# One fixed order from the first loads to the first values, a larger VectorE share of the modulation, and RMS norms two tiles at a time

## The chip, the cores and the metric

The kernel runs on one core of one Trainium2 chip. The metric is device time in microseconds (us) of one launch, from runs on the chip; less is better. The core has five instruction queues that run in order and meet through semaphores: TensorE (PE), VectorE (DVE), ScalarE (ACT), GpSimd (POOL) and SyncE (SP, which here issues most of the transfers).

## The reference, cut to what matters

A hybrid decoder block on `x` (1, 2048, 1024) in float32. The part at issue is its beginning:

```python
c_act = silu(c)                                   # (1, 1024)
mod = c_act @ w_mod + b_mod                       # (1, 3072): shift, scale, gate
h = rms_norm(x, g_norm) * (1.0 + scale) + shift   # (2048, 1024)
proj = h @ w_in                                   # 8 x 1024 columns, "v" among them
```

After that come a causal convolution with a gated linear recurrence, an attention of three dilated windows, a gated merge, an output projection with a gated residual, and a last RMS norm.

## The kernel before, in words

Positions are handled in four banks of 512 (`x0`, `x1` and so on, each four tiles of 128 rows by 1024 columns), two banks to a half `f`. Channels are on partitions in `h` (eight blocks `k` of 128), so every block of `x` is normed by rows, transposed on PE against an identity matrix and then scaled and shifted by a per-partition `gs` and `sh`. Products are made from three matmuls each (`mm3`): operands are split into a rounded part ("hi", written by ACT) and the rest ("lo", a subtraction on DVE or POOL), and hi*hi + hi*lo + lo*hi are added up in PSUM.

The stages of the first half are: the prologue (norm of `x0`, modulation, the operands `B11` and `B21` made of `x0`); the "values" (`v` = `h @ w_in` for four column groups `m` of 256 and the two banks, 96 matmuls of 128x256 for each group and bank; the norm of `x1` and its operands are made meanwhile); a long stage with the recurrence, the gates and the other projections; then the same for the second half; then attention and the output.

The prologue works in four steps `j`, each of 256 columns of shift (`q` = 0) and scale (`q` = 1):

- `load_mod(j)` loads two tiles of 1 MB (`w_m[q, j]`, eight input blocks by 256 columns) on the SP queue.
- For the first `KV` of the eight input blocks DVE multiplies the block by its column of `ca` (silu of `c`) and adds it to `acc` (one `tensor_scalar`, then `scalar_tensor_tensor`, L607 and L609). The other blocks go to PE as matmuls of one output row (`X<-T,ca`), and one more matmul with a column of ones adds up `acc` over the partitions (`X<-acc,ones`).
- ACT copies that row to SBUF (`mrow`, L615), four tiny matmuls turn it into columns (`pg<-ones,mrow`), and DVE makes `mod` (L627) and `gs` (L628) of it.
- `build` for the blocks `k` = 2j and 2j+1: four transposes on PE (L489), hi and a full copy `hf` on ACT (L492, L495), lo on DVE (L163).

Ahead of the steps are 30 idle matmuls on `busy`, the transpose of all small parameters (`prow` to `par`, L567, L568), the sigmoid of `c` (L571), and `norm_x`, which for each of the four tiles does a sum of squares on ACT, `rstd` (small operations on DVE and a square root on ACT) and the scaling by it on DVE (L478). 4, 4 and 10 more idle matmuls follow the turned rows of steps 0 to 2.

The order on each engine up to attention comes from a scheduler that works with a timeline of its own; `tc.issue_after(...)` ties some instructions behind others (L594, L603, L623, L633, L635, L637, L673). From attention on, `tc.manual_schedule()` takes the program's order. The weights of the values go through five raw buffers `R` (`NRAW`) and seven split buffers `S` (`NS`), hi by ACT (L154) and lo by POOL (L160).

Of the kernel before, what the change touches and what calls it, by code (L numbers as in the profile page):

```python
# [38 lines left out]
KV = 4  # L39
# [47 lines left out]
def decoder_block(ctx, tc, x, c, positions, g_norm, w_mod, b_mod, w_in, b_gate, conv_w, conv_b,  # L87
# [55 lines left out]
    last_mm = [None]  # L143

    def mm(o, l, r, st, sp, **kw):
        last_mm[0] = nc.tensor.matmul(o, lhsT=l, rhs=r, start=st, stop=sp, **kw).ins  # L146
# [18 lines left out]
    def rstd(ss):  # L165

        v, y, t = ss[:, 0:1], ss[:, 1:2], ss[:, 2:3]
        nc.vector.tensor_scalar(v, v, 1.0 / D, EPS, ALU.mult, ALU.add)
        nc.scalar.activation(y, v, AF.Sqrt)
        nc.vector.reciprocal(y, y)  # L170
# [33 lines left out]
    pair_id, last_hi, last_load, last_lo, last_copy = {}, [None], [None], [None], [None]  # L204
# [214 lines left out]

    def load_wv_half(m, k):  # L420

        wh = s_tile([P, KH, 2 * P])
        wl = s_tile([P, KH, 2 * P])
        for k2 in range(0, KH, 2):
            t = raw_tile([P, 2, 2 * P])
            rows = slice((k + k2) * P, (k + k2 + 2) * P)
            last_load[0] = nc.sync.dma_start(
                t[:], wcol(4 * D + m * 2 * P, 2 * P)[rows].rearrange("(k p) m -> p k m", p=P)).ins
            hi_act(wh[:, k2 : k2 + 2], t[:])
            lo_pool(wl[:, k2 : k2 + 2], t[:], wh[:, k2 : k2 + 2])  # L430
        return wh, wl
# [32 lines left out]
    def load_x(pool, n, tag, bufs):  # L464
        xs = []
        for r in range(0, 4, 2):
            t = T(pool, [P, 2, D], F32, tag, bufs=bufs)
            last_load[0] = nc.sync.dma_start(t[:], xv[n, r : r + 2].rearrange("r j d -> j r d")).ins
# [3 lines left out]
    def norm_x(st, xs, nb=2):  # L472
        for t in xs:
            jk = T(st, [P, D], BF16, "hf", bufs=nb)
            ss = T(st, [P, 4], F32, "ss", bufs=4)
            nc.scalar.activation(jk[:], t, AF.Square, accum_out=ss[:, 0:1])
            rstd(ss)
            nc.vector.tensor_scalar(t, t, ss[:, 1:2], None, ALU.mult)  # L478
# [3 lines left out]
    def build(st, names, xs, k, first=False, keep=None, spare=True):  # L482

        hh, hl = B[names[k // KH]]
        n_built[0] += 1

        pt = T(pj, [P, 4, P], F32, "Y") if spare and n_built[0] % 3 == 0 else T(pg, [P, 4, P], F32, "pg")
        for r in range(4):
            nc.tensor.transpose(pt[:, r, :], xs[r][:, k * P : (k + 1) * P], ident)  # L489
# [15 lines left out]
    def build_even(st, xs, ks=range(KT), first=False, spare=True):  # L505
        for k in ks:
            build(st, ("B11", "B21"), xs, k, first, spare=spare)
# [48 lines left out]
    idle_matmuls(30)  # L556
    nc.scalar.dma_start(cs[:], cst[:, :N_CST_A])
    prow = T(vx, [P, P], F32, "prow")

    rows = lambda v: v.rearrange("(k p) -> k p", p=P)  # L560
    for i, (r0, ap) in enumerate((
# [4 lines left out]
    pt = T(pg, [P, CH], F32, "pg")  # L566
    nc.tensor.transpose(pt[:, :N_PAR], prow[:N_PAR, :], ident[:N_PAR, :N_PAR])  # L567
    nc.vector.tensor_copy(par[:], pt[:, :N_PAR])  # L568

    ca = T(cp, [P, KT], F32, "ca")  # L570
    ca_act = nc.scalar.activation(ca[:], par[:, C_C : C_C + KT], AF.Sigmoid).ins  # L571
    nc.vector.tensor_tensor(ca[:], ca[:], par[:, C_C : C_C + KT], ALU.mult)

    norm_x(vx, x0)
    operand("B11")
    operand("B21")
# [5 lines left out]
    w_m, ws0 = {}, []  # L582
# [7 lines left out]
    for j in range(4):  # L590
        load_mod(j)
        if j == 1:

            with tc.issue_after(ca_act):  # L594
                ws0.append(load_wv_half(0, 0))
    pm_ins, gs_ins, acc_ins = [], [], []
    for j in range(4):


        pr = pj_tile([P, 2, 256])  # L600
        with ExitStack() as order:
            for ins in pm_ins[-1:] + gs_ins[-2:-1] + acc_ins[-1:]:
                order.enter_context(tc.issue_after(ins))  # L603
            for q in range(2):
                t = w_m[q, j]
                acc = T(vx, [P, 256], F32, "acc", bufs=4)
                nc.vector.tensor_scalar(acc[:], t[:, 0, :], ca[:, 0:1], None, ALU.mult)  # L607
                for k in range(1, KV):
                    acc_ins.append(nc.vector.scalar_tensor_tensor(acc[:], t[:, k, :], ca[:, k : k + 1], acc[:],  # L609
                                                                  ALU.mult, ALU.add).ins)  # L610
                for k in range(KV, KT):
                    mm(pr[:1, q, :], ca[:, k : k + 1], t[:, k, :], q == 0 and k == KV, False, skip_group_check=True)
                mm(pr[:1, q, :], ones[:, 0:1], acc[:], False, q == 1, skip_group_check=True)
        row = T(vx, [1, 2, 256], F32, "mrow", bufs=1)
        nc.scalar.activation(row[:], pr[:1], AF.Copy)  # L615
        pm = T(pg, [P, 2, 2], F32, "pg")
        for q in range(2):
            for i in range(2):
                mm(pm[:, q, i : i + 1], row[:, q, i * P : (i + 1) * P], ones[:1, 0:1],
                   q == 0 and i == 0, q == 1 and i == 1, skip_group_check=True)  # L620
        pm_ins.append(last_mm[0])
        if j < 3:
# [978 lines left out]
```

## Time and profile before

| | us |
|---|---|
| median of 3 runs | 2337.65 |
| lowest, highest | 2332.69, 2343.75 |
| the profiled execution | 2338.7 |
| its span | 2336.9 |
| PE busy in the span | 2246.0 (96%) |
| DVE, ACT, POOL busy | 1347.5, 1206.0, 952.1 |

The span runs from the first to the last recorded instruction, so 1.8 us of the profiled execution lie around it. Times in the rows below are from the start of the span. A row of the timeline has start and duration, engine, line, operation, output<-inputs, shape, count of instructions merged, and in brackets the idle time of the engine before it and what ended it. PEld is the loading of PE's stationary operand. A float32 matmul that the kernel issues once for `ca` or `ones` shows as two matmuls in the trace.

### The profile page before, as it was taken

The numbers are of one execution on the slowest core, as the hardware profiler recorded it, in microseconds if no ns is written. First come the engines' busy times: TensorE is split into PE (matmuls) and PEld (weight loads), VectorE is DVE, ScalarE is ACT, GpSimd is POOL, SyncE is SP. The second block draws the span as 40 slices with busy tenths as digits, with TensorE's granted clock in tenths as the row PEclk, the third lists the DMA queues.
The fourth block names the chain that finished last, engine by engine and source line by source line (L and its number), as shares of the span: only waits on it lengthen the run. The fifth ranks groups of instructions, "written<-read, shape, count | busy, mean of one in ns | idle before, by whom it ended". The sixth has DMA issues, their size and how long they took to land.

```text
span 2336.9 us, 34037 instructions
## 1 busy us (share of the span) xinstructions
PE 2246.0 (96%) x11461; PEld 1872.0 (80%) x11461; DVE 1347.5 (58%) x2442; ACT 1206.0 (52%) x2391; POOL 952.1 (41%) x734
## 2 busy tenths in 40 slices
PE   8998999899989999999999999999999898989998
PEld 4996777677777998787888877888889797978887
DVE  4737666756676534544434472366666777658443
ACT  4636656665643635555444411567768787634111
POOL 2456556665545533332211120446565656433000
PEclk9999999999999999999999999999999999999999
DMA  7375777676778759999677778989987887799532
GB/s 263 108 237 205 277 265 262 239 243 246 242 246 268 227 174 327 311 325 322 227 231 225 234 250 269 301 245 266 279 254 247 236 245 238 221 310 281 179 122 95
DMA packets 427284, 569.21 MB, mean 244 GB/s; under 512 B 71942, under 2 KB 292834, under 8 KB 426084
## 3 DMA queue, kind: packets, MB, share of 16 engines
q1 hardware_dynamic: 389268, 447.27, 62.2%
q10 hardware_dynamic: 37648, 119.70, 13.3%
q8 instruction: 91, 1.49, 0.3%
q14 instruction: 85, 0.70, 0.1%
q0 software_dynamic: 192, 0.05, 0.0%
HBM read 355.08 MB, written 211.82 MB: 243 GB/s over the span
## 4 chain that ended last, share of the span: by engine, by line
PE 50%; DMA 8%; DVE 4%; ACT 3%; issue 3%; POOL 2%; SPq 1%; ACTq 0%; POOLq 0%; DVEq 0%
PE pj L146 11%; PE pq L146 7%; PE X L146 6%; PE V L146 6%; PE o L146 4%; PE sc L146 4%; PE Z L146 3%; PE W L146 3%; PE Y L146 2%; PE pT L1217 1%; DMA wD<-s 1%; PE pT L1230 1%; PE pg L146 1%; DMA vraw<-vN 1%; DVE yl L163 1%
## 5 line engine op out<-in xcount | busy, mean ns | idle before, releaser
L146 PE MATMUL pj<-yh,S 128*128 128x512 f32 x1024 | 372.0, 408 | 6.1 <-DMA S<-wD 3.2
L146 PE MATMUL V<-T,S 128*128 128x512 f32 x1344 | 334.3, 397 | 12.0 <-ACT t L809 5.2
L160 POOL TENSOR_TENSOR S<-R,S 128x512 fp32r<-128x512 f32 x168 | 241.8, 1455 | 253.8 <-ACT S L200 79.2
L146 PE MATMUL X<-T,S 128*128 128x512 f32 x1344 | 332.4, 395 | 1.2 <-ACT t L888 1.2
L146 PEld LDWEIGHTS V<-T,S 128*128 128x128 f32 x1344 | 252.6, 189 | 75.9 <-ACT t L809 7.2
L146 PEld LDWEIGHTS X<-T,S 128*128 128x128 f32 x1344 | 252.4, 188 | 61.8 <-ACT t L888 2.1
L146 PEld LDWEIGHTS pj<-yh,S 128*128 128x128 f32 x1024 | 195.6, 191 | 44.0 <-DVE fg L1424 3.6
L146 PE MATMUL pj<-yl,S 128*128 128x512 f32 x512 | 203.0, 397 | 0.0
L1133 ACT ACTIVATE pp<-pp,st 128x256 f32<-128x256 f32 (+3 forms) x256 | 133.9, 524 | 113.4 <-DVE st L1132 112.7
L146 PE MATMUL W<-T,S 128*128 128x512 f32 x672 | 174.1, 404 | 0.0
L146 PE MATMUL Y<-T,S 128*128 128x512 f32 x672 | 168.6, 398 | 2.1 <-DVE t L418 2.1
L146 PE MATMUL Z<-T,S 128*128 128x512 f32 x672 | 167.4, 397 | 0.0
L146 PEld LDWEIGHTS W<-T,S 128*128 128x128 f32 x672 | 130.3, 194 | 32.4 <-issue 0.9
L146 PEld LDWEIGHTS Y<-T,S 128*128 128x128 f32 x672 | 127.0, 190 | 33.3 <-DVE t L418 2.5
L146 PEld LDWEIGHTS Z<-T,S 128*128 128x128 f32 x672 | 127.5, 190 | 30.2
L160 POOL TENSOR_TENSOR S<-s,S 128x512 fp32r<-128x512 f32 x84 | 114.9, 1369 | 77.7 <-ACT S L200 55.0
L163 DVE TENSOR_TENSOR ptl<-pT,pth 128x384 fp32r<-128x384 f32 (+1 forms) x160 | 97.8, 628 | 64.8 <-ACT pth L154 62.6
L1197 ACT ACTIVATE pp<-pp,M 128x256 f32<-128x256 f32 (+3 forms) x256 | 117.9, 523 | 8.7 <-DVE M L1321 8.6
L1132 DVE CUSTOM_DVE_ANT_0 pp<-sc,msk 128x256 f32<-128x256 f32 (+3 forms) x256 | 105.1, 449 | 30.0 <-PE sc L146 27.2
L779 DVE SCALAR_TENSOR_TENSOR xc<-xr,par,xc 128x512 f32<-128x512 f32 x96 | 84.8, 883 | 56.5 <-ACT xc L773 55.6
L160 POOL TENSOR_TENSOR kq<-kraw,kq 128x512 fp32r<-128x512 f32 (+1 forms) x64 | 101.1, 1590 | 22.9 <-ACT kq L154 22.9
L160 POOL TENSOR_TENSOR vh<-vraw,vh 128x256 fp32r<-128x256 f32 (+1 forms) x64 | 67.2, 1050 | 105.1 <-ACT vh L154 99.4
(358 smaller groups left out, 4697.7 us busy)
## 6 DMA issues: line engine op xcount, KB each, us to landing
sD<-S ACTq DMA_DIRECT2D x196, 512.0 KB, 4.2
S<-sD SPq DMA_DIRECT2D x196, 512.0 KB, 5.0
S<-wD SPq DMA_DIRECT2D x99, 512.0 KB, 5.5
R<-in_w_in_dram SPq DMA_DIRECT2D x136, 256.0 KB, 3.9
wD<-s ACTq DMA_DIRECT2D x64, 256.0 KB, 5.5
T<-in_w_mod_dram SPq DMA_DIRECT2D x8, 1024.0 KB, 11.5
vN<-ev SPq DMA_DIRECT2D x64, 128.0 KB, 2.7
zaT<-ev SPq DMA_DIRECT2D x32, 256.0 KB, 4.5
```

The lines of the kernel that those rows point to most:

```text
L146: last_mm[0] = nc.tensor.matmul(o, lhsT=l, rhs=r, start=st, stop=sp, **kw).ins
L160: nc.gpsimd.tensor_tensor(o, i, h.bitcast(F32), ALU.subtract)
L163: return nc.vector.tensor_tensor(o, i, h.bitcast(F32), ALU.subtract).ins
L779: nc.vector.scalar_tensor_tensor(xc, xr[:, i : i + CH], cw(i), xc, ALU.mult, ALU.add)
L1132: nc.vector.tensor_tensor_reduce(pdst, s_ps, mask, 1.0, 3e38, ALU.add, ALU.min, m_)
L1133: nc.scalar.activation(pdst, pdst, AF.Exp, bias=m_, scale=-1.0, accum_out=l_)
L1197: nc.scalar.activation(pp, pp, AF.Copy, scale=w)
L1217: nc.tensor.transpose(pt[:, c0 + j * P : c0 + (j + 1) * P], pp[i][:, k * P : (k + 1) * P], ident)
L1230: nc.tensor.transpose(pt[:, c * P : (c + 1) * P], pp[:, half * P : (half + 1) * P], ident)
```

## The change

1. `KV` goes from 4 to 5: of the eight input blocks of each modulation tile, DVE now sums five and PE three.
2. From the first idle matmuls to the end of the values of `m` = 0 of the first bank, the order on all engines is the program's (`tc.manual_schedule()`); the `issue_after` ties there are gone. The sums of a step for `q` = 0 come ahead of the builds of the step before, and those for `q` = 1 behind them; the transposes of step `j` stand between its row sums.
3. The values of `m` = 0 are issued in parts inside steps 2 and 3 (12, 12 and 24 matmuls for the first four blocks), and the other 48 behind the last step.
4. `c` alone is transposed first and its sigmoid taken between the squares of the first and the second pair of tiles; all parameters are transposed later. Idle matmuls are 16 and 8 instead of 30, 4, 4 and 10.
5. The raw loads of the value weights are issued apart from their splits; one more of them (`raws[1, 0]`) stands ahead of the first wait for a free buffer, and `x1` is loaded behind two more.
6. `norm_pair` takes one `rstd` for two tiles, in all places where `x` is normed. In `rstd`, one operation with two scalars and one with one become a product and an operation with two scalars.
7. The norm of `x1` is tied behind the last full copy of the prologue's builds.

```diff
-KV = 4
+KV = 5
...
-        nc.vector.tensor_scalar(t, t, v, -0.5, ALU.mult, ALU.mult)
-        nc.vector.tensor_scalar(t, t, 1.5, None, ALU.add)
+        nc.vector.tensor_tensor(t, t, v, ALU.mult)
+        nc.vector.tensor_scalar(t, t, -0.5, 1.5, ALU.mult, ALU.add)
...
+    def norm_pair(st, xs, nb=2):
+        ss = T(st, [P, 3, 2], F32, "ss", bufs=4)
+        for i, t in enumerate(xs):
+            jk = T(st, [P, D], BF16, "hf", bufs=nb)
+            nc.scalar.activation(jk[:], t, AF.Square, accum_out=ss[:, 0, i : i + 1])
+        rstd(ss)
+        for i, t in enumerate(xs):
+            nc.vector.tensor_scalar(t, t, ss[:, 1, i : i + 1], None, ALU.mult)
...
-    idle_matmuls(30)
...
+    def row_sums(j, q):
+        if q == 0:
+            pr[j] = pj_tile([P, 2, 256])
+        t = w_m[q, j]
+        acc = T(vx, [P, 256], F32, "acc", bufs=4)
+        nc.vector.tensor_scalar(acc[:], t[:, 0, :], ca[:, 0:1], None, ALU.mult)
+        for k in range(1, KV):
+            nc.vector.scalar_tensor_tensor(acc[:], t[:, k, :], ca[:, k : k + 1], acc[:], ALU.mult, ALU.add)
+        for k in range(KV, KT):
+            mm(pr[j][:1, q, :], ca[:, k : k + 1], t[:, k, :], q == 0 and k == KV, False, skip_group_check=True)
+        mm(pr[j][:1, q, :], ones[:, 0:1], acc[:], False, q == 1, skip_group_check=True)
...
+    with tc.manual_schedule():
+        idle_matmuls(16)
+        pc = T(pg, [P, CH], F32, "pg")
+        nc.tensor.transpose(pc[:, :KT], prow[:KT, :], ident[:KT, :KT])
+        cc = T(vx, [P, KT], F32, "cc")
+        nc.vector.tensor_copy(cc[:], pc[:, :KT])
...
+        squares(0)
+        nc.scalar.activation(ca[:], cc[:], AF.Sigmoid)
+        nc.vector.tensor_tensor(ca[:], ca[:], cc[:], ALU.mult)
+        rstd(norm[0])
+        scale_x(0)
+        squares(1)
+        idle_matmuls(8)
+        pt = T(pg, [P, CH], F32, "pg")
+        nc.tensor.transpose(pt[:, :N_PAR], prow[:N_PAR, :], ident[:N_PAR, :N_PAR])
+        nc.vector.tensor_copy(par[:], pt[:, :N_PAR])
+        rstd(norm[1])
+        row_sums(0, 0)
+        scale_x(1)
...
+        for j in range(4):
+            if j:
+                row_sums(j, 0)
+                build_x(j - 1)
+            if j == 2:
+                for k in range(0, KH, 2):
+                    split_wv(ws0[0], k, raws.pop((0, k)))
+                raws[1, 2] = load_wv_raw(1, 2)
+                raws[1, 4] = load_wv_raw(1, 4)
+                x1 = load_x(hp, 1, "T", 14)
+            if j == 3:
+                for k in range(KH, KT, 2):
+                    split_wv(ws0[1], k - KH, raws.pop((0, k)))
+                raws[1, 6] = load_wv_raw(1, 6)
+                first_values(0, 1, range(KH))
+            turn_x(2 * j)
+            row_sums(j, 1)
+            row(j)
+            turn_x(2 * j + 1)
+            if j == 2:
+                pv0 = [pj_tile([P, 2, 256]) for g in range(2)]
+                first_values(0, 0, range(KH))
+            if j == 3:
+                for r in range(2):
+                    first_values(1, r, range(KH))
+            turn_row(j)
+        build_x(3)
+        ws1 = [[s_tile([P, KH, 2 * P]) for l in range(2)]]
+        for k in range(0, KH, 2):
+            split_wv(ws1[0], k, raws.pop((1, k)))
+        for ks in (range(KH, KH + 2), range(KH + 2, KT)):
+            for g in range(2):
+                for r in range(2):
+                    first_values(g, r, ks)
...
+            for g in range(2):
+                store_values(vx, 0, n0, g, pv0[g])
+            with tc.issue_after(last_copy[0]):
+                norm_x(vx, xs)
```

`turn_x(k)` makes the four transposes of block `k`, `row(j)` the copy to `mrow`, `turn_row(j)` the four tiny matmuls, `mod` and `gs`, `build_x(j)` hi, `hf` and lo of the blocks 2j and 2j+1, `first_values(g, r, ks)` three matmuls for each block in `ks`.

More of the change, by code (lines that the diff above doesn't have):

```diff
@@ L503, in operand, with build_even @@
         B[name] = (slot(), slot())
-    def build_even(st, xs, ks=range(KT), first=False, spare=True):
+    def build_even(st, xs, ks=range(KT), spare=True):
         for k in ks:
-            build(st, ("B11", "B21"), xs, k, first, spare=spare)
+            build(st, ("B11", "B21"), xs, k, spare=spare)
     def build_odd(st, xs):
@@ L588, in load_mod, with turn_x, row, turn_row @@
             nc.sync.dma_start(t[:], w_mod[0, :, c0 : c0 + 256].rearrange("(k p) m -> p k m", p=P))
[L590 to L615, printed above, removed]
+    def row_sums(j, q):
[9 more added lines that the diff above has]
+        mm(pr[j][:1, q, :], ones[:, 0:1], acc[:], False, q == 1, skip_group_check=True)
+    def turn_x(k):
+        px[k] = turned(x0, k, T(pj, [P, 4, P], F32, "Y") if k % 2 else T(pg, [P, 4, P], F32, "pg"))
+    def row(j):
+        px["row"] = T(vx, [1, 2, 256], F32, "mrow", bufs=1)
+        nc.scalar.activation(px["row"][:], pr[j][:1], AF.Copy)
+    def turn_row(j):
         pm = T(pg, [P, 2, 2], F32, "pg")
```

133 lines of the change are left out of this document (73 added, 60 removed).

## The prediction

> **What bounds the kernel now.** I read the page's busy shares first, then busy time in stretches of 60 us, then the timeline of the first 100 us engine by engine, and last the clock around PE's longer pauses. The stretches have start and end, length, busy time and count of PE, PEld, DVE, ACT and POOL, the granted clock, the DMA share and GB/s.
>
> ```profile
> PE 2246.0 (96%) x11461; PEld 1872.0 (80%) x11461; DVE 1347.5 (58%) x2442; ACT 1206.0 (52%) x2391; POOL 952.1 (41%) x734
> ...
> 0.00:60.00 60.00, 52.41 (x275) 29.41 (x276) 30.23 (x84) 29.20 (x48) 14.68 (x19) 0.94 0.79 262
> 60.00:120.00 60.00, 58.33 (x489) 57.67 (x488) 44.19 (x100) 39.54 (x70) 24.38 (x15) 1.00 0.40 113
> ```
>
> PE is busy for 96% of the span, 52.4 of the first 60 us and 58.3 of the next. So time gained or lost in the prologue goes, for the most part, to the end one for one: all that follows is fed by PE's stream. The change touches some 70 of 2337 us, and 0.5% of the time, about what a measurement of this kernel can tell from no change, is 11.7 us.
>
> What does PE do in the prologue, and from when is it useful?
>
> ```profile
> 1.46 9.44 PE L146 MATMUL V<-busy 128*128 128x512 bf16 x30 [1.46 <-DVE htail L724]
> 17.45 3.52 PE L146 MATMUL X<-T,ca 128*1 128x256 f32 x8 [0.82 <-DVE ca L572]
> 21.25 1.89 PE L146 MATMUL X<-T,ca 128*1 128x256 f32 x8
> 28.35 0.59 PE L146 MATMUL Z<-acc,ones 128*1 128x256 f32 x2
> 39.31 0.66 PE L489 MATMUL Y<-cs,T 128*128 128x128 f32 x4
> 40.12 1.05 PE L146 MATMUL pg<-ones,mrow 1*128 1x1 f32 x8
> 41.10 2.33 PE L146 MATMUL V<-busy 128*128 128x512 bf16 x10
> ...
> 48.20:61.70 13.50, 11.98 (x96) 11.63 (x97) 0.00 (x0) 2.83 (x5) 5.52 (x4) 1.00 0.46 145
> ...
> 82.37 5.35 PE L146 MATMUL V<-S,T 128*128 128x256 f32 x43
> 91.41 0.99 PE L146 MATMUL X<-S,T 128*128 128x256 f32 x6 [1.29 <-POOL S L160]
> ```
>
> Idle matmuls, row sums, transposes, turned rows; the last row sums end at 48.2. From there PE is packed: of the instructions that touch the split weights `S` (the row of the stretch) it has done 96 by 61.7, as many as the values of one group need. In a packed run one matmul takes 0.12 us (5.35/43). That is the **yardstick: the 96th value matmul, before at 61.7**. The next wait is 1.29 us at 91.4, for POOL's splits.
>
> Until 48.2 it is PE that paces the steps, with 18 idle matmuls between them (0.23 each, about 4 us), and the data on its heels: DVE's first operation on the later tiles waits for the transfer until 21.46 and, for the last tile, until 36.04. The changed order loads the modulation tiles in the same sequence, with the same two raw loads among them, so these times hold after as well.
>
> ```profile
> 21.46 0.35 DVE L607 TENSOR_SCALAR acc<-T,ca 128x256 f32<-128x256 f32 x1 [0.77 <-DMA T<-in_w_mod_dram]
> 26.31 0.16 DVE L628 SCALAR_TENSOR_TENSOR gs<-mod,par 128x2 f32<-128x2 f32 x1
> 33.61 0.16 DVE L627 TENSOR_TENSOR mod<-pg,par 128x4 f32<-128x4 f32 x1 [0.30 <-PE pg L146]
> 33.80 0.16 DVE L628 SCALAR_TENSOR_TENSOR gs<-mod,par 128x2 f32<-128x2 f32 x1
> 36.04 0.35 DVE L607 TENSOR_SCALAR acc<-T,ca 128x256 f32<-128x256 f32 x1 [1.81 <-DMA T<-in_w_mod_dram]
> 42.10 0.16 DVE L628 SCALAR_TENSOR_TENSOR gs<-mod,par 128x2 f32<-128x2 f32 x1
> 52.77 0.16 DVE L628 SCALAR_TENSOR_TENSOR gs<-mod,par 128x2 f32<-128x2 f32 x1
> ```
>
> The L628 rows give the second mark of each step, the end of `gs`: 26.5, 34.0, 42.3 and 52.9.
>
> **The change part by part.** PE loses 24 of 48 idle matmuls, 18 of them between the steps, and eight row matmuls (16 rows of 1.89/8 = 0.24, 3.8 us): nearly 8 us of PE work less behind 24 us. But the fixed order makes another chain the pacemaker. DVE now has, in this order, `gs` of step j-1, the sums for `q` = 0, the two lo's of the build, and the sums for `q` = 1; before, it did both sums of a step interleaved, ahead of the builds, as soon as the tile was there. Being in order, all of that waits behind `mod`, which waits for PE, which waits for ACT's row, which waits for the last sum: the steps no longer overlap.
>
> ```profile
> 7.72 1.04 ACT L476 ACTIVATE hf<-T 128x1024 bf16<-128x1024 f32 x1
> 8.88 1.28 ACT L169 ACT_TABLE_LOAD   x1
> 10.40 0.16 DVE L170 RECIPROCAL ss<-ss 128x1 f32<-128x1 f32 x1 [1.36 <-ACT ss L169]
> 11.45 0.75 DVE L478 TENSOR_SCALAR T<-T,ss 128x1024 f32<-128x1024 f32 x1
> 16.68 0.28 DVE L568 COPY par<-pg 128x120 f32<-128x120 f32 x1 [0.95 <-PE pg L567]
> 31.88 0.59 ACT L615 ACTIVATE mrow<-Z 1x512 f32<-1x512 f32 x1 [0.43 <-PE Z L146]
> 32.02 1.28 DVE L163 TENSOR_TENSOR T<-hf,T 128x512 fp32r<-128x512 f32 x2
> 34.00 0.78 ACT L492 ACTIVATE T<-Y,mod,gs 128x512 fp32r<-128x512 f32 x1 [1.53 <-DVE gs L628]
> 34.68 0.77 ACT L495 ACTIVATE hf<-Y,mod,gs 128x512 f32<-128x512 f32 x1
> 36.80 1.32 ACT L154 ACTIVATE S<-R 128x512 fp32r<-128x512 f32 x2
> ...
> L609 DVE SCALAR_TENSOR_TENSOR acc<-T,ca,acc x24: 475/479/1490, 18.0 to 39.9; 128x256 f32<-128x256 f32 x24
> ```
>
> Prices: a sum for one `q` is 0.35 plus four `scalar_tensor_tensor` of 0.48 (the median of the last row). Each needs the one before; the dependent pair at 33.61 and 33.80 shows 0.03 between end and start, so 0.51 each and 2.4 in all. Two lo's take 1.3, ACT's four operations of a build 0.67 each start to start, row copy 0.6, PE's sum of `acc` 0.6, transposes of a block 0.6, turned row 1.05, `mod` and `gs` 0.35, a handover 0.05.
>
> *Step 0.* The first squares end at 8.88, where the table load of the row stands. Then in order: sigmoid table 1.28, sigmoid, `ca` and the first `rstd` operation 0.2 each, square root's table 1.28, root 0.2, five small DVE operations at 0.2, two scalings 1.45: 14.7. The first squares of the second pair end meanwhile, at 14.35. `par` 0.3, then mean, root and five small operations 1.4: 16.4. Sums 2.4, scalings 1.5, sums 2.4: 22.7. With PE's sum, row, turned row, `gs` and handovers 2.8: **25.5**, against 26.5.
>
> *Step 1.* 2.4 + 1.3 + 2.4 on DVE and 2.8 behind: 8.95, so **34.45**, against 34.0. PE's work fits beside it.
>
> *Steps 2 and 3* have two things more. One is a **collision of DVE and POOL**:
>
> ```profile
> 17.97 2.46 DVE L609 SCALAR_TENSOR_TENSOR acc<-T,ca,acc 128x256 f32<-128x256 f32 x6
> 21.73 4.47 DVE L609 SCALAR_TENSOR_TENSOR acc<-T,ca,acc 128x256 f32<-128x256 f32 x6
> 22.94 2.98 POOL L160 TENSOR_TENSOR S<-R,S 128x512 fp32r<-128x512 f32 x2 [18.41 <-ACT S L154]
> 37.50 3.60 POOL L160 TENSOR_TENSOR S<-R,S 128x512 fp32r<-128x512 f32 x2 [11.59 <-DMA R<-in_w_in_dram]
> ```
>
> Six of DVE's sums took 2.46 us without POOL, and 4.47 while POOL did two subtractions: 2.0 us more. One sum took 1.49 at most (row above). In the changed order the splits of the first weights stand behind the builds of step j-1 on ACT: builds until 37.2, splits (1.32 for two) until 38.4, so POOL subtracts from 37.8 to 41.4, and DVE's second sum of step 2, at 38.2, falls into it; step 3 likewise. Bounds: nothing (POOL waits instead), and 2.6 (one subtraction in front of each of two sums); I take the row's 2.0 in each step. The Trainium skill, SBUF — State Buffer, Who interferes with whom, says that a DVE instruction with two SBUF inputs and a GpSimd one that reads SBUF exclude each other for a whole instruction; the 1.49 agrees, and by that rule the price would be nearer to the upper bound.
>
> The other is what stands ahead of the turned row on PE: a block's transposes (0.6) and the new value matmuls, 12 in step 2 (1.4) and 24 in step 3 (2.9). They are useful work, but the chain waits for them; the row copy hides under them. Step 2: 6.15 + 2.0 + 0.6 + 0.6 + 1.4 + 1.05 + 0.35 = 12.15, **46.6** against 42.3. Step 3: the same with 2.9, 13.6, **60.2** against 52.9.
>
> By then 48 of the 96 matmuls are done. Blocks 4 and 5 follow at once, 24 matmuls, until 62.7. ACT builds blocks 6 and 7 until 62.95, the last lo is there at 63.65, about 18 matmuls are left: **the 96th at 65.8, against 61.7: 4.1 us late.**
>
> *The rest.* POOL splits the weights of the next group from 63.6, 1.3 to 1.8 us each, and PE uses 12 matmuls (1.4 us) of each from 65.8 on: nothing, at most 0.7. SP issues `x1` behind two raw loads that wait for POOL's subtractions in step 2, so at about 41; its norm stands behind four splits, with squares from 65 on and scaled tiles from about 70 to 72. PE turns the first of it at 68.23 (last row below), 4 us later after, at about 72: nothing, at most 1. Norms by pairs save seven small operations for every second tile; they lie beside PE's values, and in the second half beside packed matmuls: nothing. The `rstd` of the output keeps its count of operations: nothing. The wait at 91.4 stays (it may go, -1.5, or double). From there to attention the order of instructions is the old one but for some tens of rows, and from attention on it is the same.
>
> ```profile
> 68.23 0.32 PE L489 MATMUL Y<-cs,T 128*128 128x128 f32 x1
> ```
>
> **Sum:** the four `gs` move by -1.0, +0.5, +4.3 and +7.3, and the matmuls done early take 3.2 off that: +4.1. On the profiled execution that is 2338.7 + 4.1 = 2342.8; this execution lies 1.05 above the median of the three, so **2341.7** on the median.
>
> **Rivals.**
>
> *It comes out faster.* Without the collision (-4.0), with sums that overlap as before (0.41 instead of 0.51 for each of 24 in the three chained steps, -2.4) and with the wait at 91.4 gone (-1.5), the sum is -3.8: 2333.8. For it: PE has 8 us less to do, and weights are asked for earlier. Against it: dependent sums can't overlap, and POOL's work is now placed on DVE's sums. Without the collision alone it is no change, 2337.7.
>
> *It comes out slower still, by the clock.*
>
> ```profile
> 223.17 1.22 PE L146 MATMUL pg<-xh,gh 128*128 128x512 f32 x2 [5.82 <-ACT xh L154]
> 336.45 3.02 PE L146 MATMUL V<-T,S 128*128 128x512 f32 x12 [2.58 <-DVE ev L418]
> ...
> 223.00:226.00 3.00, 2.83 (x7) 2.08 (x8) 0.85 (x2) 2.54 (x7) 3.00 (x3) 0.50 0.79 313
> ...
> 336.00:340.00 4.00, 3.55 (x15) 2.94 (x16) 2.05 (x4) 1.12 (x3) 2.99 (x2) 1.00 1.01 382
> ```
>
> After PE's pause of 5.8 us the granted clock is 0.50, after one of 2.6 it stays 1.00. The row at 17.45 shows the price: eight matmuls 3.52 instead of 1.89. Idle matmuls kept PE warm between the steps, and they are gone. By my walk PE's longest pause from step 1 on is the one ahead of step 2's second sum: row matmuls done at 39.5, the sum at 42.6, 3.1 us, near the row that stays warm. If it or its like pass some 3.5 to 5 us, 36 value matmuls in the chain cost 0.12 more each, 4.3, the sums and transposes of three steps (0.6 each, half as long again) 1.8, and some 12 later ones 1.4: 7.5 on top, 2349.2. The Trainium skill, TensorE: Matmul & The Clock Gate, What's actually happening, has the array go to half its clock after an idle window of about 3.4 us, which lies between the two rows; by that rule 3.1 us would just not cool it.
>
> *It doesn't matter.* The chain is as I say, but later waits (91.4, and POOL's and DMA's ones in the long stage) take it up: 2337.7.
>
> **How the numbers follow.** My forecast (late by 2 to 7 us) 0.5; faster 0.2; the clock 0.15; no effect 0.15. All but the tail of the clock's lies within 11.7 us. The three runs shown spread over 11 us, so their median may move by about 4 without any cause. The range takes the faster case's -3.8 and the clock's +7.5 with about 3 of that scatter: 2331 to 2351. Faster by over 0.5% 0.03, within 0.91, slower by over 0.5% 0.06.
>
> **What would show it.** Ends of the four `gs` near 25.5, 34.5, 46.6 and 60.2, DVE idle for PE ahead of each `mod` and PE idle for DVE ahead of each sum of `acc`; sums of over 1.4 us beside POOL in steps 2 and 3; the clock at 1.00 from 28 us on; the 96th value matmul at 65.8. It would be wrong if DVE ends its sums as early as before, if the clock reads 0.5 behind 30 us, or if a later stage moves by more than these few us.

## The result, and the profile after

| | before | after |
|---|---|---|
| median, us | 2337.65 (11 runs) | 2351.9 (11 runs) |
| lowest, highest | 2332.69, 2343.75 | 2343.34, 2359.33 |
| the profiled execution, its span | 2338.7, 2336.9 | 2359.33, 2357.6 |

The ratio of after to before is 1.0054, 95% interval 1.0037 to 1.0072: slower by 12.6 us (8.6 to 16.8), where 4.1 were predicted. The medians lie 14.25 apart, and after's is 0.9 us above the end of the range (2351); the ratio puts the time at 2350.3. The profiled execution is the slowest of after's eleven, so its later part says little; I use its first 160 us, and for the whole time the ratio.

After, busy shares, and then the two stretches of 60 us as in the prediction (start and end, length, busy time and count of PE, PEld, DVE, ACT, POOL, clock, DMA share, GB/s):

```profile
PE 2244.4 (95%) x11422; PEld 1871.0 (79%) x11422; DVE 1350.1 (57%) x2403; ACT 1203.8 (51%) x2383; POOL 953.0 (40%) x734
```

```profile
0.00:60.00 60.00, 43.28 (x194) 21.72 (x194) 31.74 (x75) 21.52 (x34) 8.61 (x15) 0.86 0.77 253
60.00:120.00 60.00, 56.49 (x462) 55.99 (x461) 47.62 (x89) 42.37 (x72) 19.44 (x14) 0.97 0.34 100
```

PE was busy for 52.4 and 58.3 us in these stretches before: 9 us less in the first, 2 less in the second, and the clock fell from 0.94 and 1.00 to 0.86 and 0.97. The second mark, the ends of `gs` (L621 here), and the sums of step 2, from after's timeline of DVE:

```profile
25.81 0.16 DVE L621 SCALAR_TENSOR_TENSOR gs<-mod,par 128x2 f32<-128x2 f32 x1
...
34.53 0.16 DVE L621 SCALAR_TENSOR_TENSOR gs<-mod,par 128x2 f32<-128x2 f32 x1
34.61 0.35 DVE L598 TENSOR_SCALAR acc<-T,ca 128x256 f32<-128x256 f32 x1
34.99 2.05 DVE L600 SCALAR_TENSOR_TENSOR acc<-T,ca,acc 128x256 f32<-128x256 f32 x4
...
38.16 1.37 DVE L598 TENSOR_SCALAR acc<-T,ca 128x256 f32<-128x256 f32 x1
39.56 2.92 DVE L600 SCALAR_TENSOR_TENSOR acc<-T,ca,acc 128x256 f32<-128x256 f32 x4
...
48.09 0.16 DVE L621 SCALAR_TENSOR_TENSOR gs<-mod,par 128x2 f32<-128x2 f32 x1
...
61.36 0.16 DVE L621 SCALAR_TENSOR_TENSOR gs<-mod,par 128x2 f32<-128x2 f32 x1
```

POOL meanwhile, in the same execution:

```profile
38.12 2.53 POOL L158 TENSOR_TENSOR S<-R,S 128x512 fp32r<-128x512 f32 x2 [33.59 <-ACT S L152]
```

`gs` ends at 25.97, 34.69, 48.25 and 61.52 (predicted 25.5, 34.45, 46.6, 60.2). The first sum of step 2 takes 0.35 + 2.05, the second, beside POOL's two subtractions, 1.37 + 2.92: 1.9 us more, in steps 2 and 3 alike. The yardstick, in after's stretch for tile `S`:

```profile
43.40:67.10 23.70, 13.38 (x96) 12.52 (x97) 0.00 (x0) 3.99 (x7) 4.71 (x4) 0.86 0.28 103
```

The 96th value matmul is done near 67.1 instead of 61.7: 5.4 late, 4.1 predicted. Where the other 1.3 come from stands in after's timeline of PE:

```profile
42.54 0.59 PE L144 MATMUL W<-acc,ones 128*1 128x256 f32 x2 [2.89 <-DVE acc L600]
...
43.48 2.59 PE L144 MATMUL X<-S,T 128*128 128x256 f32 x12
46.00 1.86 PE L144 MATMUL pg<-ones,mrow 1*128 1x1 f32 x8
47.79 2.72 PE L144 MATMUL X<-T,ca 128*1 128x256 f32 x6
...
51.18 1.69 PE L144 MATMUL X<-S,T 128*128 128x256 f32 x12
...
83.56 0.44 PE L492 MATMUL pg<-cs,T 128*128 128x128 f32 x2 [3.47 <-DVE T L486]
```

and in its stretches of 3.41 us:

```profile
40.46:43.87 3.41, 1.33 (x9) 0.89 (x10) 1.92 (x4) 0.59 (x1) 0.19 (x1) 1.00 0.85 263
43.87:47.28 3.41, 3.41 (x17) 3.19 (x17) 0.00 (x0) 0.00 (x0) 0.00 (x0) 0.50 1.00 406
47.28:50.70 3.42, 3.27 (x10) 1.13 (x11) 2.62 (x8) 2.41 (x4) 0.00 (x0) 0.50 0.23 98
```

The pause of 2.89 us is followed by a clock of 0.50, from 43.87 to 50.70: twelve value matmuls take 2.59 us (1.69 in step 3) and the turned row 1.86 (1.05).

The last row of PE's timeline is a second loss: `x1`'s transposes wait 3.47 us for its scaling. DVE, after, in order:

```profile
72.56 0.17 DVE L739 TENSOR_TENSOR e<-e,e 128x8 f32<-128x8 f32 x1
...
76.36 1.41 DVE L486 TENSOR_SCALAR T<-T,ss 128x1024 f32<-128x1024 f32 x2
77.68 1.27 DVE L741 TENSOR_TENSOR e<-e,e 128x8 f32<-128x8 f32 x1
...
78.99 1.22 DVE L742 TENSOR_SCALAR e<-par 128x8 f32<-128x8 f32 x1
...
80.24 1.18 DVE L743 SCALAR_TENSOR_TENSOR e<-e,e 128x8 f32<-128x8 f32 x1
...
81.45 1.20 DVE L744 TENSOR_SCALAR sp<-e 128x8 f32<-128x8 f32 x1
...
82.75 1.42 DVE L486 TENSOR_SCALAR T<-T,ss 128x1024 f32<-128x1024 f32 x2
```

and POOL:

```profile
77.64 4.98 POOL L158 TENSOR_TENSOR S<-R,S 128x512 fp32r<-128x512 f32 x4 [3.73 <-PE W L144]
```

Four operations on eight columns each, 0.17 us where they run alone (the first line), took about 1.2 each, the length of one POOL subtraction (4.98/4 = 1.25): DVE and POOL take turns. They make the gates' constants, which nobody wants soon, and the scaling of `x1`'s second pair stands behind them. The operations of `rstd` on two columns that stand between the four were not held; they took 0.15 each.

A third mark sums up the first 160 us. One row of PE's timeline, twelve `V<-T,S` ahead of eight `Y<-T,S`, is in every kernel; before:

```profile
155.97 2.94 PE L146 MATMUL V<-T,S 128*128 128x512 f32 x12
```

after:

```profile
164.42 2.94 PE L144 MATMUL V<-T,S 128*128 128x512 f32 x12
```

**8.4 us late.** That leaves 4.2 of the 12.6 for all that follows, with an uncertainty as large.

### The profile page after: what moved, and what is told of

Read it like the earlier page. It is cut to its first block, busy times and chain, and to the rows that moved or that the text cites. A ratio compares the mean times of both kernels' runs of the same rounds, so it can differ in the third digit from the quotient of the medians.

```text
span 2357.6 us, 33905 instructions
## 1 busy us (share of the span) xinstructions
PE 2244.4 (95%) x11422; PEld 1871.0 (79%) x11422; DVE 1350.1 (57%) x2403; ACT 1203.8 (51%) x2383; POOL 953.0 (40%) x734
## 4 chain that ended last, share of the span: by engine, by line
PE 51%; DMA 8%; DVE 4%; ACT 2%; issue 2%; POOL 2%; SPq 1%; ACTq 0%; DVEq 0%; POOLq 0%
PE pj L144 11%; PE pq L144 7%; PE X L144 7%; PE V L144 6%; PE o L144 4%; PE sc L144 4%; PE W L144 3%; PE Z L144 3%; PE Y L144 3%; PE pT L1300 1%; DMA S<-sD 1%; PE pT L1313 1%; PE pg L144 1%; DMA vraw<-vN 1%; DMA kT<-t 1%
## 5 line engine op out<-in xcount | busy, mean ns | idle before, releaser
L144 PEld LDWEIGHTS X<-T,S 128*128 128x128 f32 x1344 | 253.1, 189 | 62.1 <-ACT t L971 1.8
L161 DVE TENSOR_TENSOR ptl<-pT,pth 128x384 fp32r<-128x384 f32 (+1 forms) x160 | 97.8, 628 | 66.6 <-ACT pth L152 64.4
```

The source lines that it names most:

```text
L161: return nc.vector.tensor_tensor(o, i, h.bitcast(F32), ALU.subtract).ins
```

## The experiments

My theory after reading the traces: the prologue's chain (sums on DVE, their collision with POOL's splits, the values ahead of the turned row, the cooled PE), and then `x1`'s norm held up. The rivals: the norm by pairs, PE's later order which it changes, or no more than what the prologue lost. All kernels, with the ratio to before of the same chip, the ends of `gs`, the start of the 96th value matmul (before 61.59, after 67.04) and the start of the row at 156 us less before's:

| kernel | ratio, 95% | us from ratio | ends of `gs` | 96th | row at 156 |
|---|---|---|---|---|---|
| after | 1.0054 (1.0037 to 1.0072) | +12.6 | 26.0 34.7 48.3 61.5 | 67.0 | +8.4 |
| e1 pairs alone | 1.0012 (0.9999 to 1.0025) | +2.8 | 26.4 34.5 42.1 53.5 | 62.1 | +0.4 |
| e2 singles behind | 1.0045 (1.0033 to 1.0057) | +10.5 | 25.1 33.8 47.2 60.4 | 66.0 | +9.1 |
| e3 four blocks | 1.0030 (1.0019 to 1.0041) | +7.0 | 25.1 33.3 44.6 57.3 | 62.9 | +4.3 |
| e4 splits behind row | 1.0034 (1.0021 to 1.0046) | +7.9 | 25.7 34.8 46.2 57.9 | 63.4 | +4.8 |
| e5 idle in pause | 1.0043 (1.0028 to 1.0057) | +10.0 | 26.1 34.8 46.7 61.1 | 66.7 | +9.0 |
| e6 values behind | 1.0012 (0.9999 to 1.0025) | +2.8 | 24.9 33.6 45.1 56.3 | 64.4 | +2.0 |
| e13 norm first | 1.0043 (1.0029 to 1.0057) | +10.0 | 25.6 34.3 48.0 61.2 | 66.8 | +4.4 |
| e10 all undone | 1.0034 (1.0021 to 1.0047) | +7.9 | 24.9 33.5 43.8 55.4 | 61.0 | +4.1 |
| f1 four undone | 1.0013 (1.0000 to 1.0025) | +3.0 | 26.3 34.9 44.0 54.1 | 62.2 | +3.5 |
| f2 three blocks | 1.0002 (0.9992 to 1.0013) | +0.5 | 23.9 32.0 40.9 51.4 | 59.4 | -0.3 |
| f3 old late order | 1.0012 (1.0002 to 1.0022) | +2.8 | 26.3 34.9 44.0 54.1 | 62.2 | +3.9 |
| f4 second split early | 0.9981 (0.9963 to 0.9998) | -4.4 | 23.9 32.0 40.9 51.7 | 59.4 | -4.7 |

The marks are from one execution of each kernel. How far they move by chance is seen in e2, whose prologue is after's line by line: its `gs` of step 0 ends 0.9 earlier, and all later marks of the prologue are 0.9 to 1.1 earlier. The clock fell at other times there (0.50 from 11.68 to 15.10 and from 18.51 to 21.92, in after from 13.15 to 23.39). So about 1 us at a mark is no effect of a change.

**e1: pairs alone.** Before, with `norm_pair` and the new `rstd` only.

```diff
-        for t in xs:
+        for i in range(0, 4, 2):
+            norm_pair(st, xs[i : i + 2], nb)
```

> The kernel before with the norms by pairs and the rewritten small operations, and nothing else of the change. Chain theory (the new fixed order strings the steps one behind the other, and that is the cost): the 96th value matmul stays within 1 us of 61.7, and the time within 3 us of the kernel before. Rival (the pairs let the scheduler lay out the rest of the program otherwise, and the loss behind 650 us comes from that): 4 to 6 us slower than before, lost behind 650 us.

The marks stand within 0.6 us of before's and the interval holds 1: the pairs aren't what costs in the first 160 us.

**e2: singles behind.** After, with `x1` and the later tiles normed one at a time (the reverse of the diff above).

> The changed kernel, but x is normed tile by tile again behind the prologue (the prologue itself keeps its pairs). Chain theory: the 96th value matmul stays at 67.2, PE's wait of 3.5 us for the norm of x1 near 83 us stays or halves, because the norm still begins behind the last build, and the time is 9 to 14 us above before. Rival (pairs): that wait goes wholly, the loss behind 650 us goes too, and the time is 5 to 8 us above before.

The row at 156 us is 0.7 later than after's, not earlier, and PE's wait for the scaled tiles is there too (3.54 us): the loss at `x1`'s norm has nothing to do with pairs.

**e3: four blocks.** `KV = 4` in after.

> The changed kernel with four of the eight input blocks on VectorE, as before the change, in the new order. Chain theory: two sums of 0.51 us less in each step, so the fourth gs ends at 57.4 in place of 61.5, the 96th value matmul is at 63.2 in place of 67.2, and the time is 4 us below the changed kernel, some 10 above before. Rival (PE paces the steps, as before the change): 16 row matmuls of 0.24 us more on PE, the fourth gs at 62 to 65, no gain or up to 4 us slower than the changed kernel.

The 96th matmul comes 4.2 earlier. By steps, against after: 0.9, 0.5, 2.3, 0.5 (differences of the ends of `gs`); the 0.9 of step 0 is what e2 has without four blocks. A chained sum should be worth 0.51 twice per step; in steps 1 and 3 it is worth half of that, since DVE, done sooner with the sums for `q` = 0, now waits for ACT's build (step 1 in DVE's timeline of e3):

```profile
27.93 0.69 DVE L161 TENSOR_TENSOR T<-hf,T 128x512 fp32r<-128x512 f32 x1 [0.43 <-ACT hf L508]
```

In step 2 it is worth more, because PE's pause got shorter and PE stayed warm (PE's timeline of e3):

```profile
40.61 0.59 PE L144 MATMUL W<-acc,ones 128*1 128x256 f32 x2 [2.46 <-DVE acc L600]
...
41.54 1.67 PE L144 MATMUL X<-S,T 128*128 128x256 f32 x12
```

**e4: splits behind the row.** After, with the splits of the first weights behind `row(j)` of steps 1 and 2.

```diff
-                for k in range(0, KH, 2):
-                    split_wv(ws0[0], k, raws.pop((0, k)))
...
             row(j)
+            if j in (1, 2):
+                for k in range(0, KH, 2):
+                    split_wv(ws0[j - 1], k, raws.pop((0, (j - 1) * KH + k)))
```

> The changed kernel with the two splits of the first value weights moved one step ahead, behind ACT's copy of the row of steps 1 and 2, so that POOL subtracts while VectorE waits for PE. Chain theory with the collision: 1.9 us less in each of steps 2 and 3, PE's pause in step 2 falls from 2.9 to about 1 us, the clock stays at 1.00 there and some 2 us more are saved; the 96th value matmul at 61 to 64, the time 4 to 6 us below the changed kernel. Rival (the collision only moves to the next sums): the 96th within 1 us of 67.2.

3.7 us off the 96th matmul. In step 3 both sums now run free (DVE's timeline of e4), 1.6 us off the step:

```profile
49.67 0.35 DVE L598 TENSOR_SCALAR acc<-T,ca 128x256 f32<-128x256 f32 x1
50.05 2.05 DVE L600 SCALAR_TENSOR_TENSOR acc<-T,ca,acc 128x256 f32<-128x256 f32 x4
```

Step 2 gains 2.1, though a sum of it is still held (1.44 for the first operation): the rest of the gain is the clock. And here a pause as long as after's did not cool PE (its timeline):

```profile
38.27 0.59 PE L144 MATMUL W<-acc,ones 128*1 128x256 f32 x2 [2.89 <-DVE acc L600]
...
42.75 1.67 PE L144 MATMUL X<-S,T 128*128 128x256 f32 x12
```

**e5: idle matmuls in the pause.**

```diff
         for k in range(KV, KT):
             mm(pr[j][:1, q, :], ca[:, k : k + 1], t[:, k, :], q == 0 and k == KV, False, skip_group_check=True)
+        if q == 1 and j in (2, 3):
+            idle_matmuls(12)
```

> After, with 12 idle matmuls put back into PE's pause ahead of the second sum of steps 2 and 3 and nothing else. Theory (the pause of 2.89 us cooled PE): the granted clock reads 0.95 or more from 44 to 50 us instead of 0.50, the 12 value matmuls of step 2 take about 1.7 us instead of 2.59 and the six row sums 1.5 instead of 2.72; gs of step 2 ends 1.4 to 2 us earlier (46.3 to 46.9), the 96th value matmul starts near 65.3 instead of 67.0, and the lag at 163 us is near 6.7 instead of 8.4. Rival (the chain alone sets it, the clock only follows): clock warm, but the ends of gs and the 96th matmul within 0.5 us of after's, or later since idle matmuls stand in the way. On the whole time at most -2 us, which these rounds can hardly tell.

Half right. The clock reads 1.00 from 37.6 us to the end of the prologue (0.50 just before, from 34.19), the twelve matmuls take 1.67, and `gs` of step 2 ends at 46.7, 1.6 us earlier: that is the price of the cooled PE. But the 96th gains only 0.4, since in after the second sum of step 3 had a pause of 1.43 only, and here its idle matmuls stand in the way. The sums are done at 54.48 (DVE), PE gets to them at 55.74:

```profile
53.27 2.54 PE L144 MATMUL V<-busy 128*128 128x512 bf16 x11 [0.16 <-issue]
55.74 0.59 PE L144 MATMUL X<-acc,ones 128*1 128x256 f32 x2
```

The lag at the row at 156 us is 9.0, not 6.7: PE waits 3.14 us for `x1` at 82.98, and the clock reads 0.50 from 81.98 to 88.80, twice as long as in after (84.83 to 88.24).

**e6: values behind the turned row.** `turn_row(j)` ahead of the `first_values` of steps 2 and 3.

> After, with the first value matmuls of steps 2 and 3 behind the turned row instead of ahead of it. Theory (the chain waits for them): gs of step 2 ends 1.5 to 2.5 us earlier, gs of step 3 3 to 5 us earlier (56.5 to 58.5); the displaced matmuls fall into PE's wait for the next sum, so the 96th starts 1 to 4 us earlier (63 to 66). Rival (they are only moved, and PE's time is what counts): gs earlier but the 96th at 66.5 to 67.5, and the time that of after. Further on I expect the lag to follow the 96th matmul one for one.

The chain waited for them: `gs` of step 3 ends 5.2 us earlier, the 96th matmul starts 2.7 earlier. Of both, 1.1 lie in step 0, which this change doesn't touch; steps 2 and 3 gain 2.1 and 2.0. The row at 156 us gains 6.4, more than that: in this timing the last of DVE's small operations miss POOL's subtractions (0.17 each instead of 1.2) and `x1`'s wait is gone, with no line of that part changed. The time follows: 1.0012 (0.9999 to 1.0025).

**e13: norm first.** After, with the small operations of the constants tied behind the last scaling of `x1`.

```diff
-    with tc.issue_after(last_lo[0]):
-        sp8 = T(cp, [P, 8], F32, "sp8")
+    sp8 = T(cp, [P, 8], F32, "sp8")
+
+    def make_sp8():
...
                 norm_x(vx, xs)
+            with tc.issue_after(last_scale[0]):
+                make_sp8()
```

> After, with the small operations of the gates' constants (L724 to L744 of after) tied behind the scaling of x1 on DVE. Theory (they are held 1.2 us each by POOL's subtractions, and the second pair's scaling stands behind them): PE's wait of 3.47 us near 83 us shrinks to 1 us or less, and the lag at 163 us falls from 8.4 to 5.3 to 6; the time falls by 2 to 3 us. Rival (x1 is late because its transfer and its squares are): the wait stays at 2.5 us or more and the lag at 163 us stays near 8. Until 70 us everything as in after.

As the theory has it, and 0.9 better. The scalings, in e13's timeline of DVE:

```profile
73.11 1.42 DVE L488 TENSOR_SCALAR T<-T,ss 128x1024 f32<-128x1024 f32 x2
...
75.23 1.42 DVE L488 TENSOR_SCALAR T<-T,ss 128x1024 f32<-128x1024 f32 x2
```

The second pair is scaled 7.5 us earlier than in after (82.75), PE's wait is gone, and the row at 156 us is 4.0 earlier while the 96th is 0.3 earlier: **3.7 us is what `x1`'s norm cost** with the constants in its way. Not all of the 7.5 is POOL's doing: the first pair too is scaled 3.25 earlier (76.36 in after), because the constants' exponential, with its table load and the root's behind it (1.28 us each on ACT, at 68.51 and 73.60 in after), is out of the way as well. The other 4.3 are the four held operations. e6 has the table loads ahead of the root but no held operation between the two scalings, and no wait for `x1`. The whole time fell by 2.6, which the intervals alone could not tell.

**e10: all undone.** After, with e3, e4 and e2 together and the counter of built tiles started at 8 (`n_built = [8]`), which gives PE's later order of before but for some twenty rows.

> After, with four tiles on DVE again, the splits of the first weights behind the row copies of steps 1 and 2, x1 and the later tiles normed one at a time, and the counter of built tiles started at 8 so that the later order of PE's instructions is that of before but for some twenty rows. Theory: gains add up, 4.2 for the tile and 3.7 for the splits: the 96th value matmul starts at 59 to 60.5 (before 61.6), and the lag at 163 us is 1 to 3 (singles added 4.7 between the two marks in the kernel with single norms); and if the later order is what costs between 650 and 870 us, the lag moves there by 1.5 us or less (after +4.6, four tiles +5.0, splits +6.0, singles +3.2): time 2336 to 2340 beside 2336 of before. Rival (the loss between 650 and 870 us has nothing to do with the order of PE's instructions): it is 3 us or more here too, and the time is 2340 to 2343.

The 96th starts at 61.0, 0.6 ahead of before and half a microsecond later than expected at most, and the row at 156 us is 4.1 late, because `x1`'s wait is there again (3.52 us at 78.49 in PE's timeline of e10).

The time, 1.0034 (1.0021 to 1.0047), fits neither theory about the later order: the trace loses only 1 us between 650 and 870 us, as that theory has it, and yet the time is no lower than the row at 156 us and 3.8 us more.

**f1: four undone.** After with e3, e4, e6 and e13; the pairs stay.

> After with four things changed together: four tiles on DVE, the splits of the first weights behind the row copies of steps 1 and 2, the first values behind the turned rows, and the gates' constants behind the scaling of x1; the norm by pairs stays. Theory (the prologue's chain sets after's time, and each of the four takes its part off): the 96th value matmul starts at 57 to 60 (before 61.6), the lag at 163 us is -3 to 0, PE has no wait over 1.5 us between 62 and 110 us, and the time lies 0 to 4 us above before's, 2334 to 2339, because about 2 us stay lost behind 640 us in all kernels with the norm by pairs. Rival (a bound of another kind, transfers or PE's own work, lies just below): the 96th not under 60.5 and the lag at 163 us over 1; time 2339 or more.

The gains don't add up: the 96th at 62.2, as the rival has it. Steps 1 to 3 are short (8.6, 9.2, 10.1 us), but PE was cold for step 0 and again at 34 us (two stretches of f1):

```profile
30.83:34.25 3.42, 2.72 (x18) 1.59 (x17) 0.92 (x3) 1.62 (x3) 0.68 (x1) 1.00 1.10 346
34.25:37.66 3.41, 3.11 (x8) 0.68 (x6) 3.27 (x6) 2.77 (x4) 1.81 (x2) 0.50 0.97 296
```

Eight row sums took 3.36 there instead of 1.89. No pause of PE over 0.55 us stands in the 8 us before it.

**f2: three blocks.** f1 with `KV = 3`.

> The same with three tiles on DVE instead of four. Theory (DVE's chained sums pace the steps, 0.51 us each, two per step): 8 sums fewer take up to 4 us off the gs of step 3 against the kernel with four, while PE gets 8 row sums more (1.9 us). I expect about -2 at the 96th matmul. Rival (with four tiles PE or the transfers of the modulation already pace the steps): within 0.7 us of the kernel with four, or later by up to 2. Time within 2 us of the kernel with four, so it is read from the trace.

2.8 us off the 96th, but not as the theory has it: 2.35 of it are in step 0, where PE was warm this time; the three chained steps gain 0.4 together. With four blocks PE's own work paces them already. Then 2.7 us are given back; PE's timeline of f2:

```profile
90.24 1.32 PE L144 MATMUL X<-S,T 128*128 128x256 f32 x6 [2.70 <-POOL S L158]
...
92.21 4.47 PE L144 MATMUL X<-S,T 128*128 128x256 f32 x29
```

What PE waits for is one POOL subtraction, and that one is itself held up. POOL, in f2 and in before:

```profile
83.93 6.26 POOL L158 TENSOR_TENSOR S<-R,S 128x512 fp32r<-128x512 f32 x1 [8.57 <-PE V L144]
```

```profile
86.53 4.83 POOL L160 TENSOR_TENSOR S<-R,S 128x512 fp32r<-128x512 f32 x1 [7.44 <-PE V L146]
```

Such a subtraction takes 1.3 us alone. Here eight operations of DVE on two tiles each, 0.68 us long (84.17 to 89.06 in f2, the build of `x1`'s operands), run ahead of it without a break. It is the collision of steps 2 and 3 with the roles changed, and it is also what the wait at 91.4 of before, and the one of 2.71 in f1, come from.

**f3: old late order.** f1 with singles and `n_built = [8]`.

> The kernel with four things changed, and besides x1 and the later tiles normed one at a time with the counter of built tiles at 8, so that PE's later order is that of before but for some twenty rows. Theory (norm by pairs moves the later order and so costs some 2 us between 650 and 745 us): lag there +1.2 or less instead of about +2, and the whole time 1 to 3 us under the kernel with pairs, which the interval can just tell; if the sums come out, 2332 to 2336, level with before or a little faster. Rival (that late difference is scatter between executions): the time is that of the kernel with pairs within 1 us.

The rival: 1.0012 (1.0002 to 1.0022) beside 1.0013 (1.0000 to 1.0025), with all marks of the prologue the same. The norm by pairs and PE's later order make no difference that these runs can tell.

**f4: second split early.** f2, with the first half of the second group's splits behind the row copy of step 3.

```diff
+            if j == 3:
+                ws1 = [[s_tile([P, KH, 2 * P]) for l in range(2)]]
+                for k in range(0, KH, 2):
+                    split_wv(ws1[0], k, raws.pop((1, k)))
...
         build_x(3)
-        ws1 = [[s_tile([P, KH, 2 * P]) for l in range(2)]]
-        for k in range(0, KH, 2):
-            split_wv(ws1[0], k, raws.pop((1, k)))
```

> The kernel with three tiles on DVE, with the first half of the second group's splits behind the row copy of step 3 on ACT instead of behind the last builds. Theory (the lead of 2.7 us at 75 us is given back at the wait of 2.70 us for POOL's splits near 90 us, because the raw tiles come free late and SP's loads behind them with them): the splits run from about 48 us instead of 54, the loads follow some 5 us earlier, the wait near 90 us falls to 1 us or less, and the lag at 163 us is -2 to -3; time 2332 to 2335 beside 2335.7 of before, which the interval may just tell from no change. Rival (that wait is set by the transfers of the next group's weights, not by when they are asked for): wait and lag as in the kernel with three tiles, 2.7 and -0.3 us.

The wait goes and the lag is -4.7, more than expected, but not by the way of the theory. The splits do run earlier; POOL's timeline of f4 (in f2 four subtractions began at 54.77, here two of them run ahead):

```profile
50.45 2.52 POOL L158 TENSOR_TENSOR S<-R,S 128x512 fp32r<-128x512 f32 x2 [8.30 <-ACT S L152]
55.22 2.55 POOL L158 TENSOR_TENSOR S<-R,S 128x512 fp32r<-128x512 f32 x2 [2.26 <-ACT S L152]
```

But the subtraction that PE waited for in f2 starts no earlier (83.93 there); it is released by PE in both, so neither the loads nor the transfers set it. It only isn't held:

```profile
83.97 1.52 POOL L158 TENSOR_TENSOR S<-R,S 128x512 fp32r<-128x512 f32 x1 [7.72 <-PE V L144]
```

From here on the two engines alternate, DVE 1.77 and POOL 1.74 us for each operation. Which of them goes first at 84 us, and whether the earlier splits decide it, is not shown. A stretch of f4:

```profile
80.00:90.00 10.00, 10.00 (x87) 10.00 (x86) 10.00 (x13) 5.13 (x9) 6.03 (x4) 1.00 0.28 80
```

PE is packed without a wait, and warm; the 29 matmuls that took 4.47 in f2 (PE's timeline of f4):

```profile
88.60 3.61 PE L144 MATMUL X<-S,T 128*128 128x256 f32 x29
```

The row at 156 us gains 4.4: the 2.70 of the wait, 0.9 in this row, and 0.8 around them. The median is 2333.41 beside 2339.29 of before on the same chip, ratio 0.9981 (0.9963 to 0.9998): the one version whose interval lies below 1, and only just. One in twelve is weak evidence by itself; the earlier row in the trace supports it.

## Why the prediction came out as it did

The direction and the cause of the first 4 us were right; the size was a third of the whole.

- *Step 0 and step 1*: 25.97 and 8.72 us, predicted 25.5 and 8.95. Right, as near as step 0 can be told (25.1 in e2 with the same prologue).
- *The collision*: 1.9 us in each of steps 2 and 3, predicted 2.0; e4 takes it out of step 3 and the step gains 1.6. Right in size, though it held one `scalar_tensor_tensor` and the `tensor_scalar` ahead of it, not two sums. The Trainium skill, SBUF — State Buffer, Who interferes with whom, names `tensor_scalar` among the operations that can take both ports and so exclude GpSimd; the 1.37 instead of 0.35 agrees.
- *The values ahead of the turned row*: predicted 1.4 and 2.9 in the chain; e6, by taking them out, gains 2.1 in step 2 and 2.0 in step 3. Right in the sum, and dearer in step 2, where PE was cold. That most of it is no loss for the 96th matmul is right: of e6's 2.7 there, 1.1 lie in step 0, so 1.6 of some 4 us were lost.
- *Step 2* took 13.56 us instead of 12.15. **The failed step is the clock**: I put the pause ahead of the second sum (3.1 by my walk, 2.89 measured) "near the row that stays warm". It cooled PE, for 1.6 us by e5. The rival "by the clock" happened, but in the prologue only in step 2: 1.6, not its 7.5.
- *To the 96th matmul*: 13.27 us for step 3 and 5.6 behind it, predicted 13.6 and 5.6. Right; with the clock the sum gives 5.4 late.
- *`x1`'s norm*: "nothing, at most 1". **Wrong**: 3.7 by e13. I had counted the squares and the two scalings, not the queues that they stand in: on DVE the small operations for the constants, four of which are held for one POOL subtraction each, and on ACT the table loads for their exponential. The bound had to be the length of POOL's run that can fall ahead of the scaling: four subtractions, 5 us. The trace of before shows the hold on two of these operations, 1.25 us at 58.22 and this one (DVE, before):

```profile
65.61 1.22 DVE L660 TENSOR_SCALAR e<-e 128x8 f32<-128x8 f32 x1
```

- *The wait at 91.4*: predicted to stay; it went in after (1.3 us in its favour), where the same four subtractions start at 96.75 and take 6.87 us in all instead of 9.93. I had taken it for POOL's splits being late; it is one subtraction that DVE holds up, 4.83 us long in before and 6.26 in f2.
- *Norm by pairs, later order*: costed at nothing; e1 and f3 agree within what they can tell.
- *Behind the row at 156 us*: costed at nothing. Over the thirteen kernels of the table the time from the ratio is on average 1.9 us above the lag at that row (spread 2.0), so the two run together, and f4's sign follows it. What these 1.9 us are is **open**. One candidate is seen in the traces, the same hold of POOL in the second half; POOL's timeline, before:

```profile
814.99 3.93 POOL L160 TENSOR_TENSOR S<-R,S 128x512 fp32r<-128x512 f32 x1 [8.90 <-ACT T L154]
```

and after:

```profile
826.89 5.34 POOL L158 TENSOR_TENSOR S<-R,S 128x512 fp32r<-128x512 f32 x1 [8.66 <-ACT hx L508]
```

PE's wait behind it is 0.36 us in before and 1.79 in after. f4 is the only kernel of the table in whose first 1000 us no subtraction of POOL's takes over 3 us. It was not tried by itself.

So of the 12.6 us, 5.4 are the chain with the cooled PE, 3.0 lie between the 96th matmul and the row at 156 us (3.7 for `x1`'s norm, less 0.7 that after gains on before in this part without it, the gone wait at 91 among them), and 4.2, with an uncertainty as large, were not found. The fixed order itself isn't to blame: f2 keeps it, with other places for the splits, the first values and the constants and with three blocks on DVE, and is level with before (1.0002, 0.9992 to 1.0013).

## What to carry to other kernels

In an order written by hand, ask of every instruction that another waits for what stands ahead of it on its queue, also what is small and not urgent, and price each that can meet a run of POOL's at one POOL instruction (1.25 us here for work of 0.17). Work that is useful but not urgent (values, splits, constants) goes behind the handover that the chain waits for, not ahead of it. Where an engine waits for an operation of another, look first at how long that operation itself took: f2 gave all of its lead back at one subtraction of 6.26 us that DVE held up, and f4 kept it where the same subtraction, begun at the same time, took 1.52.

## What the runs showed of the hardware

- A DVE operation on 128x8 values takes 0.17 us alone and 1.18 to 1.27 when it is held by one of POOL's subtractions of 1.25, also with a single SBUF input and constants (1.20, L744). In after's run of four subtractions four of eight small operations were held; the other four, on 128x2 values, took 0.15.
- DVE can hold POOL as well, and for longer than one operation: a subtraction of 1.3 us took 6.26 in f2 beside eight DVE operations of 0.68 on two tiles each, 4.83 in before (86.53) and 5.34 in after (826.89). In these three the hold ended where a DVE operation had to wait 0.03 to 0.04 us for the result of the one before it.
- The length of a pause does not decide whether PE cools: 2.89 us did in after and not in e4, 2.70 did in f2 (the 29 matmuls at 92 us), 2.46 did not in e3, and in f1 the clock fell at 34 us behind no pause over 0.55. The clock changes at steps of 3.41 us only: all stretches at 0.50 in the first 110 us of the fourteen traces last 3.41, 6.83 or 10.24. Counted over the fourteen traces, a warm step behind which the clock fell has PE busy for 1.86 us at most, and one behind which it stayed for 1.50 at least, with three exceptions near 31 us (e5, f1, f3: 2.3 to 2.7 us, 1.5 to 1.7 of it transposes and turned rows). That these count for less would explain f1; it was not tried. The Trainium skill, TensorE: Matmul & The Clock Gate, What's actually happening, says that activity is watched in a free-running window of about 3.4 us; the steps and the unequal outcome of equal pauses agree. Its table there has PE cool after an idle window; here steps with up to 1.86 us of work did it too, and 3.4 us of idleness were not needed. In after 2.08 us of the pause lie in one step, in which PE is busy for 1.33 us; in e4 the equal pause, 35.38 to 38.27, lies across two:

```profile
33.41:36.82 3.41, 1.97 (x12) 0.91 (x11) 2.69 (x5) 2.53 (x5) 2.48 (x2) 1.00 1.07 336
36.82:40.24 3.42, 1.97 (x11) 0.84 (x11) 3.28 (x8) 0.77 (x2) 0.00 (x0) 1.00 0.85 261
```

- Idle matmuls put into a pause keep PE warm (e5: 1.00 from 40 to 54 us), but where the pause turns out shorter than they are they delay the chain, by 1.3 us in step 3 of e5.
